# A two-layer encoder kernel: a thirteenth feed-forward chunk by seven half-size products, shared PSUM banks, x kept in DRAM, some low parts added by DMA out of HBM

## The chip, the cores and the metric

The kernel runs on one core of one Trainium2 chip. A core has a matrix engine (TensorE, PE in the profile; its weight loads are PEld), VectorE (DVE), ScalarE (ACT), GpSimd (POOL) and SyncE (SP), which work side by side, each on a queue of its own in order, and 16 DMA engines. Data lie in HBM (also called DRAM here), in the core's SBUF, and in PSUM, eight banks of 128 x 512 fp32 values into which TensorE writes. The metric is the device time of one execution in microseconds (us), the median of several; lower is better.

## What is computed

x is 512 tokens by 1024 features, in fp32. Two layers follow each other; the first mixes tokens by a gated linear attention (GLA), the second by softmax attention with rotary positions. Each mixer is followed by a feed-forward part:

```python
for i in range(DEPTH):                      # 2
    h = rmsnorm(x, norm_mix[i])
    x = x + (gla_mixer(h, ...) if i % 2 == 0 else attn_mixer(h, ...))
    x = x + conv_ffn(rmsnorm(x, norm_ffn[i]), ffn_w_up[i], ffn_w_conv[i], ffn_b_conv[i], ffn_w_down[i])

def conv_ffn(h, w_up, w_conv, b_conv, w_down):      # w_up 1024 x 5632, w_down 2816 x 1024
    u = conv3(h @ w_up, w_conv) + b_conv            # depthwise over tokens, width 3
    val, gate = split(u, 2)
    return (silu(gate) * val) @ w_down
```

## The kernel before

**Precision.** Every fp32 operand of a matmul is held as a high part, rounded to the matrix engine's fp32r form, and a low part, the rest. One product is three matmuls: high x high, high x low, low x high (`mm3`, lines 387 to 389, and the loop at 856 and 857). The high part of a weight is a ScalarE copy (line 227), the low part a VectorE subtraction (line 228). `low_dma` (lines 178 to 181) makes the low part in another way: ScalarE writes the high part (179), then its negative, the raw value negated and rounded, into the low tile (180), and an accumulating DMA issued by POOL adds the raw value (`flush`, line 217).

**Tiling.** Features lie on the 128 partitions, 512 tokens on the free axis: x is eight tiles of 128 x 512. The 5632 up-projection features are 22 chunks m, each with a value and a gate tile. A *plain* chunk (`plain_up`) is two tiles of 8 x 3 = 24 matmuls of 512 columns. A chunk in SEVEN (`seven_up`) is done by a Strassen-like scheme: four blocks of weights, token halves of 256 columns, and seven products instead of eight; each product is 4 pairs x 3 = 12 matmuls of 256 columns (`product`, line 848), so a chunk is 84. Sums of weight blocks are made by VectorE (`summed`, lines 187 to 212), sums of input blocks in `prepare_input`. Results are put together in PSUM banks r1 to r5 and the SBUF tiles c and d: ScalarE copies r2<-r1 (line 873) and r3<-r2 (877), VectorE adds. In before, 12 chunks are done this way.

**Down-projection.** 16 of the 22 chunks feed it by seven products as well, in two parts after chunks 9 and 17 (`down_part`), of four strips with 84 matmuls each. Their inputs are pairs of chunks (`prepare`); the pairs in Q_DMA get their low parts by accumulating DMA, the others by VectorE (line 919). The results g and f of a strip are added to x in SBUF by accumulating DMA. The last six chunks are multiplied plainly at the end (PLAIN, `mm3` into `dn`).

**Activation.** `act_up` takes the two results of a chunk through the convolution (ScalarE line 904, VectorE 905 and 906), the gate's SiLU (908) and the product (909).

**Normalisation.** The first SWITCH chunks multiply the un-normalised x (tiles xhl) and are scaled by R behind the matmul (line 845). From chunk SWITCH on, the normalised x is used (tiles nh and nl, made in `rescale` with low parts by accumulating DMA). `prepare_input` runs after the chunks named in INPUT_AT and makes the tiles xt.

**Buffers.** A pool tag has a fixed number of buffers: raw weights NR = 4 (of 128 x 1024), high and low parts NH = NL = 4, u 4, t 6, sq 3; PSUM banks acc 3, s 2, pt 2, po 1. `Weights.piece` makes pieces ahead of their use, as many as PA, UPA or `ahead` say, and loads LOADS further ones ahead on SP.

**Order.** The source gives dependencies and priorities; the tile framework orders each engine's queue when the program is built, by its own cost estimates, and makes an instruction wait where a buffer or an operand is due. So the order in the trace isn't always that of the source. `issue_after` fixes an order by hand.

In the GLA part (lines 465 to 800) each head makes ktl twice (line 633, tag u), kth twice (tag t), at (t), ath and atl (658 and 659, u), then runs 18 kv matmuls and 12 o matmuls (702), copies of kv by line 690, and the next head's projections.

Of the kernel before, what the change touches and what calls it, by code (L numbers as in the profile page):

```python
# [48 lines left out]
SEVEN = (7, 8, 10, 11, 12, 13, 15, 16, 18, 19, 20, 21)  # L49
# [3 lines left out]
SWITCH = 4  # L53
INPUT_AT = {3: (0, 1), 4: (2,), 5: (3,)}
Q_DMA = (2, 4, 5, 6)
NR = 4
NH = 4
NL = 4

# [9 lines left out]
def hybrid_encoder_kernel(  # L69
# [25 lines left out]
    pp = ctx.enter_context(tc.tile_pool(name="pp", bufs=1, space=bass.MemoryType.PSUM))  # L95

# [17 lines left out]
    def tmp(tag, n, w=S):  # L114
        return sp.tile([P, w], F32, tag=tag, bufs={"u": 4, "t": 6, "sq": 3}[tag], name=nm(n))
# [5 lines left out]
    x = [cp.tile([P, S], F32, name=f"x{c}") for c in range(KC)]  # L121
    prm = cp.tile([P, PC_N], F32, name="prm")

    class Weights:
# [3 lines left out]
        def __init__(self):  # L128
            self.todo, self.made, self.by_dma, self.pending = [], {}, [], []
            self.sums, self.last, self.fine = set(), None, []  # L130
            self.loaded, self.strip = {}, {}

        def add(self, src, strips=None, pieces=2):
            for i in strips or range(src.shape[0]):
                order = (0, 1, 3, 2) if pieces > 2 and src.shape[0] == FC else range(pieces)
                self.todo += [(src, i, h) for h in order]
                if pieces > 2:
                    self.sums.add((id(src), i))
# [22 lines left out]
        def make(self, key):  # L161
# [13 lines left out]
        def two(self):  # L175
            return pair("wh", NH, F32R, "wh"), pair("wl", NL, F32R, "wl")

        def low_dma(self, hi, lo, r):
            act.activation(hi, r, AF.Copy)
            act.activation(lo, r, AF.Copy, scale=-1.0)  # L180
            self.pending.append((lo, r))

        def summed(self, src, i, h):
# [3 lines left out]
            a21, a11, a12, a22 = t1[:, :S], t1[:, S:], t3[:, :S], t3[:, S:]  # L187
            if h == 0:
                r = tmp("t", "sum")
                with tc.issue_after(self.last.ins) if self.last else ExitStack():  # L190
                    dve.tensor_tensor(r, a21, a11, ALU.add)
                    dve.tensor_tensor(a21, a21, a22, ALU.add)
                hi, lo = self.two()
                for sl, y in ((slice(0, S), r), (slice(S, 2 * S), a11)):
                    act.activation(hi[:, sl], y, AF.Copy)
                    dve.tensor_tensor(lo[:, sl], y, hi[:, sl].bitcast(F32), ALU.subtract)
                return hi, lo
            if h == 1:
                dve.tensor_tensor(a11, a21, a11, ALU.add)
                hi, lo = self.two()  # L200
                self.split(hi, lo, t1)
                return hi, lo
            if h == 2:
                hi, lo = self.two()
                self.split(hi, lo, t3)
                return hi, lo
            r = tmp("sq", "sum4")
            dve.tensor_tensor(r, a11, a12, ALU.add)
            hi, lo = (sp.tile([P, S], F32R, tag="sq", bufs=3, name=nm(n)) for n in ("wh4", "wl4"))
            act.activation(hi, r, AF.Copy)  # L210
            self.last = dve.tensor_tensor(lo, r, hi.bitcast(F32), ALU.subtract)
            return hi, lo

        def flush(self):

            for lo, r in self.pending:
                pool.dma_start(lo.bitcast(F32), r, accum_op=ALU.add)
# [23 lines left out]
        def ahead(self, n):  # L241
# [3 lines left out]
            for key in self.todo[:LOADS]:  # L245
# [36 lines left out]
    act.dma_start(prm, par)  # L282
    raw = [pair("raw", NR, F32, "first") for i in range(4)]
# [145 lines left out]
    def out_steps(src, hl, nxt, late):  # L429
# [19 lines left out]
        def end(ng):  # L449
            for n in range(2):  # L450
                c = ng * 2 + n
                dve.tensor_tensor(x[c], x[c], pss[ng][n], ALU.add)
                nxt.chunk(c)

# [10 lines left out]
    def gla(norm, nxt):  # L465
# [58 lines left out]
        rst = sp.tile([P, S], F32R, tag="t", bufs=6, name="rst")  # L524
# [77 lines left out]
        def f32r(tag, n):  # L602
            return sp.tile([P, S], F32R, tag=tag, bufs={"u": 4, "t": 6}[tag], name=nm(n))
# [770 lines left out]
```

## Time and profile before

| what | value |
|---|---|
| time, median of 3 runs | 1098.73 us (1098.07 to 1100.32) |
| the profiled execution's own time | 1098.06 us |
| its span, first to last instruction | 1096.3 us |
| granted TensorE clock | 1.000 |
| GLA and start, to the first up matmul | 0 to 225.9 us |
| feed-forward, layer 0 | 225.9 to 572.6 us |
| attention | 572.6 to 746.0 us |
| feed-forward, layer 1 | 746.0 to 1092.9 us |
| HBM read, written | 100.21 MB, 2.10 MB |

The profile is of one execution. A row of its order of time has the start, the duration, the engine, the line, the operation, what is written and read (buffer numbers left out), the shape, and in brackets the engine's idle time before it and what ended it. A group's row has the count, the busy time and mean duration in ns, and the idle time before such instructions. In a table by windows, each engine has its busy time and the number of its instructions in that stretch (PE, PEld, DVE, ACT, POOL), then the clock, the mean busy share of the DMA engines and GB/s. Matmuls overlap, so their pace is read from their starts.

### The profile page before, as it was taken

The numbers are of one execution on the slowest core, as the hardware profiler recorded it, in microseconds if no ns is written. First come the engines' busy times: TensorE is split into PE (matmuls) and PEld (weight loads), VectorE is DVE, ScalarE is ACT, GpSimd is POOL, SyncE is SP. The second block draws the span as 40 slices with busy tenths as digits, with TensorE's granted clock in tenths as the row PEclk, the third lists the DMA queues.
The fourth block names the chain that finished last, engine by engine and source line by source line (L and its number), as shares of the span: only waits on it lengthen the run. The fifth ranks groups of instructions, "written<-read, shape, count | busy, mean of one in ns | idle before, by whom it ended". The sixth has DMA issues, their size and how long they took to land.

```text
span 1096.3 us, 17577 instructions
## 1 busy us (share of the span) xinstructions
PE 1088.7 (99%) x6644; PEld 975.0 (89%) x6644; DVE 881.3 (80%) x1417; ACT 678.0 (62%) x1158; POOL 143.4 (13%) x158
## 2 busy tenths in 40 slices
PE   9999999999999999999999999999999999999998
PEld 7888888888899999999988888788889999999997
DVE  6686776669989799988955588766998979998892
ACT  6565343447766677666764677745776667766670
POOL 0100123000100211010014343000110021101000
PEclk9999999999999999999999999999999999999999
DMA  7432223236645745364457474433673574536422
GB/s 255 132 98 95 66 70 116 83 101 162 154 111 140 174 121 149 116 164 125 154 137 180 120 227 143 157 111 97 157 163 103 147 171 124 146 111 166 125 95 77
DMA packets 52309, 146.45 MB, mean 134 GB/s; under 512 B 6144, under 2 KB 7680, under 8 KB 52224
## 3 DMA queue, kind: packets, MB, share of 16 engines
q1 hardware_dynamic: 32736, 102.17, 28.5%
q0 software_dynamic: 14592, 34.61, 17.2%
q10 hardware_dynamic: 4896, 8.55, 2.1%
q8 instruction: 52, 0.85, 0.3%
q14 instruction: 33, 0.27, 0.1%
HBM read 100.21 MB, written 2.10 MB: 93 GB/s over the span
## 4 chain that ended last, share of the span: by engine, by line
PE 94%; DVE 2%; ACT 2%; issue 1%; DMA 1%; DVEq 0%; SPq 0%; ACTq 0%
PE r L857 33%; PE vg L419 8%; PE op L445 8%; PE up L387 7%; PE up L388 7%; PE up L389 7%; PE dn L387 2%; PE dn L388 2%; PE dn L389 2%; PE av L419 1%; PE o L713 1%; PE A L387 1%; PE B L387 1%; PE A L389 1%; PE B L389 1%
## 5 line engine op out<-in xcount | busy, mean ns | idle before, releaser
L227 ACT ACTIVATE wh<-raw 128x1024 fp32r<-128x1024 f32 x164 | 171.6, 1055 | 146.7 <-PE op L445 32.1
L228 DVE TENSOR_TENSOR wl<-raw,wh 128x1024 fp32r<-128x1024 f32 x164 | 199.9, 1224 | 46.4 <-ACT wh L227 43.5
L857 PE MATMUL r<-gu,wh 128*128 128x256 f32 x896 | 162.8, 284 | 0.0
L857 PE MATMUL r<-xt,wh 128*128 128x256 f32 x768 | 141.1, 284 | 1.0 <-ACT r L873 1.0
L857 PEld LDWEIGHTS r<-gu,wh 128*128 128x128 f32 x896 | 140.1, 192 | 1.6 <-ACT r L976 0.6
L857 PE MATMUL r<-gu,wl 128*128 128x256 f32 x448 | 126.5, 283 | 0.0
L857 PEld LDWEIGHTS r<-xt,wh 128*128 128x128 f32 x768 | 119.9, 192 | 2.6 <-ACT r L873 1.8
L857 PE MATMUL r<-xt,wl 128*128 128x256 f32 x384 | 108.3, 283 | 0.0
L857 PEld LDWEIGHTS r<-gu,wl 128*128 128x128 f32 x448 | 85.9, 192 | 0.0
L857 PE MATMUL r<-nl,wh 128*128 128x256 f32 x288 | 81.5, 283 | 0.0
L857 PE MATMUL r<-nh,wl 128*128 128x256 f32 x288 | 81.5, 283 | 0.0
L857 PE MATMUL r<-nh,wh 128*128 128x256 f32 x288 | 81.5, 283 | 0.0
L419 PE MATMUL vg<-wh,xhl 128*128 128x512 f32 x256 | 79.7, 390 | 1.1 <-DVE wh L225 1.1
L387 PE MATMUL up<-nh,wh 128*128 128x512 f32 x192 | 74.9, 390 | 0.0
L388 PE MATMUL up<-nl,wh 128*128 128x512 f32 x192 | 74.9, 390 | 0.0
L389 PE MATMUL up<-nh,wl 128*128 128x512 f32 x192 | 74.7, 389 | 0.0
L857 PEld LDWEIGHTS r<-xt,wl 128*128 128x128 f32 x384 | 73.5, 192 | 0.0
L445 PE MATMUL op<-oT,wh 128*128 128x512 f32 x256 | 72.1, 394 | 0.0
L419 PEld LDWEIGHTS vg<-wh,xhl 128*128 128x128 f32 x256 | 48.0, 188 | 11.2 <-ACT sq L361 1.3
L445 PEld LDWEIGHTS op<-oT,wh 128*128 128x128 f32 x256 | 47.4, 188 | 9.7 <-ACT oT L741 0.3
L857 PEld LDWEIGHTS r<-nl,wh 128*128 128x128 f32 x288 | 55.3, 192 | 0.2
L857 PEld LDWEIGHTS r<-nh,wh 128*128 128x128 f32 x288 | 55.3, 192 | 0.2
(279 smaller groups left out, 2745.2 us busy)
## 6 DMA issues: line engine op xcount, KB each, us to landing
raw<-in_w_up_dram SPq DMA_DIRECT2D x84, 512.0 KB, 3.9
raw<-in_w_down_dram SPq DMA_DIRECT2D x44, 512.0 KB, 4.1
wl<-raw POOLq DMA_DIRECT2D x16, 512.0 KB, 4.9
raw<-in_w_vg_dram SPq DMA_DIRECT2D x12, 512.0 KB, 3.9
ring<-p ACTq DMA_DIRECT2D x22, 256.0 KB, 2.9
raw<-in_w_kq_dram SPq DMA_DIRECT2D x8, 512.0 KB, 3.6
raw<-in_w_gout_dram SPq DMA_DIRECT2D x8, 512.0 KB, 3.6
nl<-xr POOLq DMA_DIRECT2D x8, 512.0 KB, 5.3
```

Source lines behind the costliest of these rows:

```text
L227: act.activation(hi[:, sl], r[:, sl], AF.Copy)
L228: dve.tensor_tensor(lo[:, sl], r[:, sl], hi[:, sl].bitcast(F32), ALU.subtract)
L387: mm(ps, wh, mh, start=start, stop=False)
L388: mm(ps, wh, ml, start=False, stop=False)
L389: return mm(ps, wl, mh, start=False, stop=stop)
L419: mm(ps[j][:, :width], hl[k][i == 2][:, j * P : (j + 1) * P], (wl if i == 1 else wh)[:, sl], start=k == 0 and i == 0, stop=k == KC - 1 and ...
L445: mm(pss[ng][n], wt[:, sl], mv, start=k == 0 and i == 0, stop=k == KC - 1 and i == 2)
L713: last = mm(og[s], l, r, start=False, stop=i == len(parts) - 1, skip_group_check=True)
L857: mm(dst, w[:, sl], m, start=start and j == 0 and a == 0, stop=j == len(pairs) - 1 and a == 2, skip_group_check=True)
```

## The change

- Chunk 6 joins SEVEN (13 chunks). SWITCH and INPUT_AT move one chunk earlier.
- The seven products use another set of block sums with other signs, so that subtractions take the place of some scaled ones. A strip's third sum is one VectorE operation of 1024 into a raw buffer; there are three splits of 1024 and one of 512.
- Results share banks: r1 and r2 are the halves of one acc bank. The first product goes to a pt bank, and ScalarE copies it into both halves (`twice`). r3 is a whole s bank, whose halves are two copies of r2 at two moments. One VectorE addition of 512 makes d. The convolution reads the other result in PSUM, and c is gone. The order of the products is 1, 6, 7, 4, 5, (1 of the next chunk), 2, 3; before it was 1, 6, 7, 3, 5, 4, (1), 2 for up chunks and 1, 6, 7, 5, 4, 3, (1), 2 for down strips.
- The low parts of the plain chunks 1, 2 and 5 are made by `low_dma`, and the accumulating DMA reads the raw weights in HBM (UP_DMA). Q_DMA is empty: the low parts of those pairs go to VectorE.
- x is saved to DRAM by SP as the mixer's output projection ends (`x_save`), and the down parts are accumulated there. Its four SBUF buffers hold every third piece of weights from chunk 1 to 20 (`wide`), with more pieces ahead (PAW = 6). At chunk 20 x is loaded back (`x_load`).
- Buffers: raw 5 for 4, u 3 for 4, t 5 for 6. In the attention, copies of probabilities go to a raw buffer, and one rotary tile to the tag R.

```diff
-SEVEN = (7, 8, 10, 11, 12, 13, 15, 16, 18, 19, 20, 21)
+SEVEN = (6, 7, 8, 10, 11, 12, 13, 15, 16, 18, 19, 20, 21)
-SWITCH = 4
-INPUT_AT = {3: (0, 1), 4: (2,), 5: (3,)}
-Q_DMA = (2, 4, 5, 6)
-NR = 4
+SWITCH = 3
+INPUT_AT = {2: (0, 1), 3: (2,), 4: (3,)}
+Q_DMA = ()
+UP_DMA = (1, 2, 5)
+NR = 5
+LOADS_FFN = 3
+WIDE_AT, BACK_AT = 1, 20
+PAW, UPAW = 6, 3
...
-        return sp.tile([P, w], F32, tag=tag, bufs={"u": 4, "t": 6, "sq": 3}[tag], name=nm(n))
+        return sp.tile([P, w], F32, tag=tag, bufs={"u": 3, "t": 5, "sq": 3}[tag], name=nm(n))
...
+    def x_save(p):
+        if p == 0:
+            x_home[:] = [dp.tile([P, 2 * S], F32, tag=nm("xd"), name=nm("xd")) for _ in range(KC // 2)]
+        for i in range(2):
+            sync.dma_start(x_home[p][:, i * S : (i + 1) * S], x[2 * p + i])
+    def x_load():
+        for home, t in zip(x_home, x_tiles()):
+            sync.dma_start(t, home)
...
+            elif any(src is a and i in UP_DMA for a in up):
+                self.low_dma(hi, lo, r, src[i, :, h * 2 * S : (h + 1) * 2 * S].bitcast(F32R))
...
         def two(self):
+            self.turn += self.wide
+            if self.wide and self.turn % 3 == 0:
+                return pair("x", KC // 2, F32R, "wh"), pair("x", KC // 2, F32R, "wl")
             return pair("wh", NH, F32R, "wh"), pair("wl", NL, F32R, "wl")
...
+            if h == 1:
+                e = pair("raw", NR, F32, "sum")
+                self.strip[id(src), i].append(e)
+                both = lambda t: t.rearrange("p (o n) -> p o n", n=S)
+                with tc.issue_after(self.last.ins) if self.last else ExitStack():
+                    dve.tensor_tensor(both(e), both(a21).to_broadcast([P, 2, S]), both(t1), ALU.subtract)
+                dve.tensor_tensor(a21, a11, e[:, S:], ALU.subtract)
+            hi, lo = self.two()
+            self.split(hi, lo, self.strip[id(src), i][h])
...
         def seven_up(m):
-            r1 = bank("acc", "r1")[:, :H]
-            go(1, r1, True)
-            r2 = bank("acc", "r2")[:, :H]
-            act.activation(r2, r1, AF.Copy)
+            r = bank("pt", "r1")[:, :H]
+            go(1, r, True)
+            both = bank("acc", "r")
+            r1, r2 = both[:, :H], both[:, H:]
+            twice(both, r)
             yield
             go(6, r2, False)
-            r3 = bank("s", "r3")[:, :H]
-            act.activation(r3, r2, AF.Copy)
+            r3 = bank("s", "r3")
+            act.activation(r3[:, :H], r2, AF.Copy)
             r4 = bank("pt", "r4")[:, :H]
             go(7, r4, True)
-            r5 = bank("pt", "r5")[:, :H]
-            go(3, r5, True)
+            d = tmp("u", "u")
+            twice(d, r4)
+            go(4, r3[:, :H], False)
             go(5, r2, False)
...
-            go(4, r3, False)
+            act.activation(r3[:, H:], r2, AF.Copy)
+            add_seven(d, r3, r4)
+            yield 1, d
             begin_up(m + 1)
             go(2, r1, False)
-            dve.tensor_tensor(d[:, :H], d[:, :H], r3, ALU.subtract)
-            yield 1, d
-            act.activation(c[:, :H], r1, AF.Copy)
-            yield 0, c
+            go(3, r2, False)
+            yield 0, both
...
+        def twice(d, r4):
+            two = lambda a: a.rearrange("p (o t) -> p o t", t=H)
+            act.activation(two(d), two(r4).to_broadcast([P, 2, H]), AF.Copy)
+        def add_seven(d, r3, r4):
+            dve.tensor_tensor(d, d, r3, ALU.add)
...
         for m in range(FC):
+            if m == BACK_AT:
+                W.loads, W.wide = LOADS, 0
+                x_load()
+            elif m == WIDE_AT:
+                W.loads, W.wide = LOADS_FFN, 1
             held.append(act_up(m))
```

`down_part` is changed in the same way as `seven_up`; there a strip's two results go by ScalarE to f and g and are accumulated into x_home.

More of the change, by code (lines that the diff above doesn't have):

```diff
@@ L131, in __init__ @@
             self.loaded, self.strip = {}, {}
+            self.loads, self.wide, self.turn = LOADS, 0, 0
         def add(self, src, strips=None, pieces=2):
             for i in strips or range(src.shape[0]):
[L135 to L136 removed]
+                self.todo += [(src, i, h) for h in range(pieces)]
                 if pieces > 2:
@@ L183, in summed @@
         def summed(self, src, i, h):
             t1, t3 = self.strip[id(src), i][:2]
[L187 to L196, printed above, removed]
+            a11, a21, a12 = t1[:, :S], t3[:, :S], t3[:, S:]
@@ L828, in plain_up @@
                 ps = bank("s" if t else "acc", "up")
-                feature_tile(*W.half(up[layer], 2 * m + t, max(UPA, ahead.get((m, t), 1))), norm.hl if m < SWITCH else fresh, ps)
+                feature_tile(*W.half(up[layer], 2 * m + t, max(UPAW if W.wide else UPA, ahead.get((m, t), 1))), norm.hl if m < SWITCH else fresh, ps)
                 pss.append(ps)
@@ L850, in product @@
             if h not in pieces:
-                pieces[h] = W.piece(src, strip, h, PA)
+                pieces[h] = W.piece(src, strip, h, PAW if W.wide else PA)
             wh, wl = pieces[h]
```

114 lines of the change are left out of this document (52 added, 62 removed).

## The prediction

> **What bounds the kernel now.** I read the page first (busy shares, then the chain that ended last), then TensorE's waits, then its order of time.
>
> ```profile
> span 1096.3 us, 17577 instructions
> ...
> PE 1088.7 (99%) x6644; PEld 975.0 (89%) x6644; DVE 881.3 (80%) x1417; ACT 678.0 (62%) x1158; POOL 143.4 (13%) x158
> ...
> PE 94%; DVE 2%; ACT 2%; issue 1%; DMA 1%; DVEq 0%; SPq 0%; ACTq 0%
> ```
>
> The chain runs through TensorE for 94% of the span: the time is the number of matmuls times their pitch, plus what TensorE waits. Waits come next; columns are who waited for whom, us in total, times, longest.
>
> ```profile
> PE r L857 <- ACT r L873: 1.0, 2, 0.5
> ```
>
> It is the only wait of note in the two feed-forward stages: once in each layer a product waits for ScalarE's copy r2<-r1. A busy row overlaps its neighbours (284 ns for a 256-column matmul), so I take the pitch from first starts in the order of time:
>
> ```profile
> 238.07 0.48 PE L387 MATMUL up<-xhl,wh 128*128 128x512 f32 x1
> ...
> 298.02 0.28 PE L857 MATMUL r<-nh,wh 128*128 128x256 f32 x1
> ...
> 336.00 0.28 PE L857 MATMUL r<-gu,wh 128*128 128x256 f32 x1
> ...
> 409.79 0.28 PE L857 MATMUL r<-nh,wl 128*128 128x256 f32 x1
> 410.60 0.39 PE L857 MATMUL r<-xt,wh 128*128 128x256 f32 x1 [0.53 <-ACT r L873]
> ...
> 416.43 0.40 PE L387 MATMUL up<-nh,wh 128*128 128x512 f32 x1
> ...
> 929.88 0.28 PE L857 MATMUL r<-nh,wl 128*128 128x256 f32 x1
> 930.68 0.39 PE L857 MATMUL r<-xt,wh 128*128 128x256 f32 x1 [0.52 <-ACT r L873]
> ```
>
> Between 238.07 and 298.02 stand plain chunks 1 to 5 and one tile of 6, 11 x 24 = 264 matmuls of 512 columns: 59.95 / 264 = 0.2271 us each. Between 336.00 and 416.43 stand four down strips and chunks 10 to 13: 8 x 84 less the 12 of the first product, done ahead, is 660 matmuls of 256 columns. The start gap at 409.79 is 0.81, which is 0.69 over a pitch of 0.12; (80.43 - 0.69) / 660 = 0.1208 us. In layer 1 the same wait costs 0.80 - 0.12 = 0.68.
>
> **The change part by part.** *Chunk 6 by seven products.* Plain: 48 x 0.2271 = 10.90 us; seven: 7 x 12 x 0.1208 = 10.15. It saves 0.75 a layer, **-1.50 us**. No other edit changes the number of matmuls, so the rest counts by waits alone.
>
> *The wait for r2<-r1.* Now ScalarE copies r1 out of its own bank into both halves of the shared one, and two products (2 and 3 of the chunk before, 2 x 1.45 = 2.9 us) lie between it and its reader, in place of one. Why it was late:
>
> ```profile
> 406.00:416.40 10.40, 9.88 (x82) 9.67 (x82) 9.54 (x17) 9.95 (x19) 2.93 (x4) 1.00 0.97 233
> ```
>
> ScalarE (the second figure of 9.9 with x19) was busy 9.95 of 10.40 us, with the negated copies of line 180 for pair 6. Q_DMA is empty now, so these go too. I count both waits gone: 0.69 + 0.68, **-1.37 us**. Next late are the copies below.
>
> *VectorE, ScalarE, POOL.* Prices:
>
> ```profile
> L228 DVE TENSOR_TENSOR wl<-raw,wh 128x1024 fp32r<-128x1024 f32 x164 | 199.9, 1224 | 46.4 <-ACT wh L227 43.5 <-issue 1.3 <-PE r L857 1.3
> L227 ACT ACTIVATE wh<-raw 128x1024 fp32r<-128x1024 f32 x164 | 171.6, 1055 | 146.7 <-PE op L445 32.1 <-DVE raw L199 30.1 <-PE up L388 26.5
> ...
> L196 DVE TENSOR_TENSOR wl<-sum,wh 128x512 fp32r<-128x512 f32 x40 | 27.5, 688 | 10.0 <-ACT wh L195 9.4
> ...
> L886 DVE TENSOR_TENSOR u<-u,r 128x256 f32<-128x256 f32 x24 | 9.9, 414 | 0.0
> ...
> L179 ACT ACTIVATE gu<-y 128x512 fp32r<-128x512 f32 x16 | 10.0, 625 | 3.4 <-DVE y L909 3.2
> ```
>
> VectorE, a layer, with 1.22, 0.69 and 0.41 us for 1024, 512 and 256 columns. Six low halves go to DMA, -7.3. Four prepared pairs return from it, 4 x (3 x 0.69 + 0.41) = +9.9. A strip costs 4 x 1.22 + 3 x 0.69 = 6.95 in place of 2 x 1.22 + 7 x 0.69 = 7.27, on 20 strips -6; chunk 6 as a strip is +4.5. Results cost one add of 512 (0.69) in place of three of 256 (1.24), -6.6 on 12 chunks, +0.7 for chunk 6, -1 on the down strips. SWITCH drops two scalings, -1.4. Sum about -7 us. ScalarE, by the 1.06 and 0.63 us rows: +6.3 for the six negated copies, -9 for the pairs, -4 on strips, +3.6 for chunk 6, -2 on results, +3.7 down: about -1. Neither is on the path while pieces are ready, and the lookahead grows from four pairs of buffers to six: **0 us**, but it is what hides these engines. POOL issues 6 accumulations more and 16 fewer a layer. x goes out and back 2 MB a layer on SP; x_load waits there until the four borrowed buffers are free and holds up the loads queued behind it, late in chunk 21, when the first down halves are in the raw buffers already: 0.
>
> *Copies with less cover.* Line 877's copy r3<-r2 had two to three products between its source (6) and its reader (4); now only product 7. And r1 and r2 share a bank. What that means shows where kv halves share one:
>
> ```profile
> 139.89 0.28 PE L389 MATMUL kv<-vrh,ktl 128*128 128x256 f32 x1
> ...
> 140.24 0.28 PE L389 MATMUL kv<-vrh,ktl 128*128 128x256 f32 x1
> ...
> 140.56 0.38 ACT L690 ACTIVATE sa<-kv 128x256 f32<-128x256 f32 x1 [0.68 <-PE kv L389]
> ```
>
> ScalarE reads the half that was done at 139.89 + 0.28 = 140.17, idles, and starts at 140.56, just after the other half's last matmul (140.24 + 0.28). So products 2 and 3 must wait for the second copy, r3's right half <- r2 after product 5, though 2 writes the other half. The Trainium skill (PSUM — Partial Sum Buffer, section "PSUM bank collisions raise a hardware error") asks for the same: guard by bank, not by address; the trace agrees, and that rule speaks against this part of the change. The price goes by bounds:
>
> ```profile
> 347.95 0.37 ACT L985 ACTIVATE r<-r 128x256 f32<-128x256 f32 x1 [0.87 <-PE r L857]
> ```
>
> Where ScalarE is waiting already, the copy follows its product at once and ends 0.37 us later, in a cover of 1.45: nothing is lost. Upper end: 13 + 8 strips in two layers with two such copies are 84. Before, 16 places a layer had one product of cover and lost 1.37 together, 0.043 each, so 76 cost 3.3; after chunks 8, 13, 16 and 21 no begun chunk covers the second copy, 8 x about 0.6 = 4.8 if nothing else is put in. But other work is put in: the queue order bends around a late operand:
>
> ```profile
> 175.91 0.28 PE L702 MATMUL o<-vrl,ath 128*128 128x256 f32 x1
> 176.03 0.28 PE L702 MATMUL o<-vrh,ath 128*128 128x256 f32 x1
> 176.26 0.39 PE L702 MATMUL o<-vrh,atl 128*128 128x256 f32 x1
> ```
>
> Here the third matmul by source order (atl) comes behind a later one with ath, since atl was late. I take **+0.2** (0 to +8.1), by the row at 347.95.
>
> *Three u tiles in place of four.* A GLA head holds four (two ktl, ath, atl). Now atl waits until the first ktl is read, by the ninth kv matmul, which is the third in front of the 139.89 row above (starts 139.53, ends 139.8). In front of it on VectorE:
>
> ```profile
> 139.64 1.22 DVE L228 TENSOR_TENSOR wl<-raw,wh 128x1024 fp32r<-128x1024 f32 x1 [0.17 <-ACT wh L227]
> ...
> 140.96 0.28 PE L702 MATMUL o<-vrh,atl 128*128 128x256 f32 x1
> ```
>
> atl would end at 140.8 + 0.69 = 141.5 and is due at 140.96: 0.55 in three heads, 1.7, less what later ath matmuls fill. If VectorE is free at 139.8 it is nothing. I take **+0.2** (0 to +1.7). The t tiles (five for six) have a free one by then.
>
> *The low parts of chunks 1, 2, 5, and SWITCH.* The critical one is the second half of chunk 2:
>
> ```profile
> 246.75 1.04 ACT L227 ACTIVATE wh<-raw 128x1024 fp32r<-128x1024 f32 x1
> ...
> 252.41 0.87 POOL L217 DMA_DIRECT2D nl<-xr  x1 [1.56 <-ACT nl L180]
> ...
> 254.96 0.39 PE L389 MATMUL up<-xhl,wl 128*128 128x512 f32 x1
> ```
>
> The first is ScalarE's high part, the second the last accumulation for the normalised x, the third the half's first use of its low part. The landing times of those accumulations (the view of the tile nl):
>
> ```profile
> DMA to landing us min/median/max: 4.6/5.3/7.5
> ```
>
> The DMA share (1.02) in that stretch, in the table by windows:
>
> ```profile
> 249.00:260.00 11.00, 11.00 (x50) 9.09 (x50) 11.00 (x18) 7.89 (x11) 1.72 (x2) 1.00 1.02 224
> ```
>
> The high part starts at 246.75, the negated copy would end at 248.8, and an accumulation issued then lands 4.6 to 7.5 us later: 253.4 to 256.3, against a first use at 254.96. The median leaves 0.8. The normalised x's low parts, due a chunk earlier by SWITCH, land last at 252.41 + 7.5 = 259.9; the last pair's first use is in chunk 3, six 128-row steps after its start: 238.07 + 96 x 0.2271 + 19 x 0.2271 = 264.2. I take **0** (0 to +8 a layer, below). HBM latency under load is up to 2 us in the Trainium skill (DMA: Bandwidth & Descriptors, section "Latency and other measured facts"); no run here shows an accumulation out of HBM. By that figure, an estimate, this half would land at about 256.1 and cost 1.2 us a layer, and the sum would be 2.4 us higher.
>
> Sum: -1.50 - 1.37 + 0.2 + 0.2 = -2.5 us on the profiled execution (1096.3 span, 1.8 around it, 1098.06 in all). The median of three is 1098.73, 0.67 above it, and the comparison is with such a median: 1098.73 - 2.5 = **1096.2 us**.
>
> **The rivals.** *The covers give it back (same).* The copies after products 6 and 5, and atl, cost 2 to 3 us of their 9.8: 1098.5. For: ScalarE's 1.06 us copies stand in the same queue and can't be interrupted. Against: only two late copies in 32 so far. That chunk 6 gains nothing (a piece of it late on a VectorE that is full from 249 to 260) ends here too: 1097.7.
>
> *The low parts land late (slower).* One mechanism: in 249 to 260 the DMA engines are full (share 1.02), and another 0.5 MB accumulation goes among four. The queue that accumulates:
>
> ```profile
> q0 software_dynamic: 14592, 34.61, 17.2%
> ```
>
> 0.172 x 1096.3 = 188.6 us for 34.61 MB, so 2.9 us for 0.52 MB. Behind the last nl it would land at 259.9 + 2.9 = 262.8, 7.8 us late; behind one or two of them, about 3. It decides from an issue later than 254.96 - 5.3 = 249.7. At 3 us a layer the time is 1102.2, at the end of the bound 1111.8. For: full engines and a slack of 0.8 us. Against: POOL could issue it at 248.8, ahead of two nl.
>
> *All covers hold (faster).* 1098.73 - 2.87 = 1095.9; runs of before lie down to 0.7 below their median (1098.07), so 1095.2.
>
> **How the numbers follow.** Forecast with all covers holding or nearly so 0.43; gain given back 0.27; low parts late or another feed missed 0.30. A difference of 0.2% (2.2 us) is about what a measurement of this kernel can tell from none. Faster 0.43, same 0.27, slower 0.30. The likeliest case's own range is 1095.2 to 1096.5. The range of 8 in 10 goes from 1094.9 to 1103.0, the slower rival at 3 us a layer and a little; beyond it stay its worst end, 0.13, and 0.05 below.
>
> **What would show it.** Right: chunk 6 takes 10.15 us; no wait of TensorE for line 873's successor. Copies: waits of product 4 or 2 for ScalarE. GLA: o waits for atl at 121, 141, 161. Low parts: TensorE's up waits for a DMA at 249 to 265 and 769 to 785. Wrong altogether: pieces late, seen as r waiting for VectorE's wl.

## The result and the profile after

| | before | after |
|---|---|---|
| median of 20 runs | 1099.81 us (1098.07 to 1100.61) | 1096.97 us (1095.75 to 1098.75) |
| the profiled execution's own time | 1098.06 us | 1096.11 us |
| its span | 1096.3 us | 1094.0 us |

The ratio is 0.9979, 95% interval 0.9973 to 0.9985: the kernel after is faster by 2.8 us, where 2.5 was forecast. (1096.2 was forecast from the first median of before, 1098.73; all 20 runs of it have 1099.81.) The runs of each kernel fall in two groups 1.6 to 1.9 us apart and the two medians lie in different groups; group by group the kernel after is faster by 2.3 us (medians 1098.49 and 1096.19) and by 2.0 us (1100.10 and 1098.13). The page of the kernel after, with the rows that answer to those of before (span; busy time by engine; the chain that ended last):

```profile
span 1094.0 us, 17377 instructions
...
PE 1086.3 (99%) x6716; PEld 975.8 (89%) x6716; DVE 870.8 (80%) x1301; ACT 683.1 (62%) x1086; POOL 126.6 (12%) x138
...
PE 96%; DVE 2%; ACT 1%; DMA 1%; issue 0%; SPq 0%; DVEq 0%; ACTq 0%
```

TensorE has 72 matmuls more (2 x 36: 84 of 256 columns for 48 of 512 in chunk 6, twice) and is busy 2.4 us less. VectorE loses 10.5 us and ScalarE gains 5; with TensorE at 99% neither shows directly. TensorE's waits in the kernel after (line waited for, us in total, times, longest):

```profile
PE r L879 <- ACT r L907: 0.7, 1, 0.7
PE o L724 <- DVE atl L681: 0.3, 2, 0.2
...
PE pt L1257 <- DMA ring<-p: 0.2, 1, 0.2
```

The old row (L857 for L873, 1.0 in two places) is gone; three new ones stand here, the last in the attention. Which stage each us came from is read from first starts in the order of time: first up matmul, first matmul of the attention, last up or down matmul. "Waits" in the table are the gaps between all starts of TensorE in a feed-forward part, each less the pitch of its width (0.227 or 0.120 us), added up.

| us | first up matmul at | layer 0 feed-forward (waits in it) | attention | layer 1 feed-forward (waits) | span |
|---|---|---|---|---|---|
| before | 225.88 | 346.69 (2.28) | 173.43 | 346.49 (2.31) | 1096.3 |
| after | 226.90 | 344.13 (0.54) | 173.63 | 345.51 (2.14) | 1094.0 |
| difference | +1.02 | -2.56 (-1.74) | +0.20 | -0.98 (-0.17) | -2.3 |

A layer's matmuls without their waits take 344.41 and 344.18 us before, 343.59 and 343.37 after: 0.8 less in each. That 0.8 is the counts times the two pitches (48 x 0.227 - 84 x 0.120), so it is no measurement of its own. This is one: in layer 0, from the first up matmul to the first product of a down strip, both kernels have the same matmuls but for chunk 6 and the same two gaps of 0.1 us, and the stretch takes 103.22 us before (225.88 to 329.10) and 102.46 after (226.90 to 329.36), 0.76 less. The rest is waits: 1.74 us of them gone in layer 0, next to none in layer 1, and 1.0 us more ahead of the feed-forward.

Layer 1 lost most of its gain in one place, shown by the order of time (start, duration, instruction; in brackets the idle time before it and what ended it). First TensorE, then ScalarE, both of the kernel after:

```profile
829.98 0.28 PE L879 MATMUL r<-nh,wl 128*128 128x256 f32 x1
830.24 0.50 PE L879 MATMUL r<-xt,wh 128*128 128x256 f32 x2
831.45 0.38 PE L879 MATMUL r<-nh,wh 128*128 128x256 f32 x1 [0.71 <-ACT r L907]
```

```profile
828.18 1.06 ACT L247 ACTIVATE wh<-raw 128x1024 fp32r<-128x1024 f32 x1 [1.21 <-DVE raw L228]
829.14 1.04 ACT L247 ACTIVATE wh<-sum 128x1024 fp32r<-128x1024 f32 x1
830.09 1.04 ACT L247 ACTIVATE wh<-raw 128x1024 fp32r<-128x1024 f32 x1
831.04 0.36 ACT L907 ACTIVATE r<-r 128x256 f32<-128x256 f32 x1
```

Product 2 waits for the second copy out of the shared bank. That copy takes 0.36 us, but stands behind three copies of a weight piece, and the first of those had waited 1.21 us for a sum from VectorE. In this queue, which runs in order, one late operand was passed on to all behind it. Layer 0 has the same program, and there this place shows no wait.

Ahead of the feed-forward the new wait is that for atl, twice the same (at 121.65 and 141.63); VectorE first, then TensorE:

```profile
120.22 1.23 DVE L248 TENSOR_TENSOR wl<-raw,wh 128x1024 fp32r<-128x1024 f32 x1 [0.17 <-ACT wh L247]
121.36 0.69 DVE L681 TENSOR_TENSOR atl<-at,ath 128x512 fp32r<-128x512 f32 x1
```

```profile
121.53 0.28 PE L724 MATMUL o<-vrh,ath 128*128 128x256 f32 x1
121.65 0.28 PE L724 MATMUL o<-vrl,ath 128*128 128x256 f32 x1
122.10 0.39 PE L724 MATMUL o<-vrh,atl 128*128 128x256 f32 x1 [0.17 <-DVE atl L681]
122.32 0.28 PE L724 MATMUL o<-vrh,ath 128*128 128x256 f32 x1
```

The start gap is 0.45, so 0.33 over the pitch, and the gap behind it 0.22 in place of 0.12: with the second head about 0.85 us, most of the 1.02.

The low parts out of HBM cost TensorE nothing. Landing times of accumulations (KB each, median us from issue to landing, DMA view of the kernel after; the third row is the normalised x's, out of SBUF and in the same stretch), the issue for the second half of chunk 2, that half's first use, and two windows: the 277 matmuls from the first up matmul on, before and after.

```profile
wl<-raw POOLq DMA_DIRECT2D x16, 512.0 KB, 5.2
...
wl<-in_w_up_dram POOLq DMA_DIRECT2D x12, 512.0 KB, 7.9
...
nl<-xr POOLq DMA_DIRECT2D x8, 512.0 KB, 7.9
```

```profile
241.02 0.88 POOL L237 DMA_DIRECT2D wl<-in_w_up_dram  x1 [5.48 <-ACT wl L206]
...
255.98 0.39 PE L410 MATMUL up<-xhl,wl 128*128 128x512 f32 x1
```

```profile
225.88:287.14 61.26, 61.26 (x277) 50.83 (x276) 54.96 (x91) 41.02 (x54) 7.15 (x8) 1.00 0.55 139
```

```profile
226.90:288.16 61.26, 61.26 (x277) 50.84 (x276) 52.71 (x90) 49.05 (x62) 12.37 (x14) 1.00 0.91 205
```

Issued at 241.02 it lands, by the median, at about 248.9, 7 us ahead of its use. The stretch takes 61.26 us in both kernels, although the DMA engines went from 0.55 to 0.91 busy.

### The profile page after: what moved, and what is told of

Same layout as the page of the kernel before. It is cut to its first block, busy times and chain, and to the rows that moved or that the text cites. A ratio compares the mean times of both kernels' runs of the same rounds, so it can differ in the third digit from the quotient of the medians.

```text
span 1094.0 us, 17377 instructions
## 1 busy us (share of the span) xinstructions
PE 1086.3 (99%) x6716; PEld 975.8 (89%) x6716; DVE 870.8 (80%) x1301; ACT 683.1 (62%) x1086; POOL 126.6 (12%) x138
## 4 chain that ended last, share of the span: by engine, by line
PE 96%; DVE 2%; ACT 1%; DMA 1%; issue 0%; SPq 0%; DVEq 0%; ACTq 0%
PE r L879 37%; PE vg L440 8%; PE op L466 8%; PE up L408 6%; PE up L409 6%; PE up L410 6%; PE dn L409 2%; PE dn L410 2%; PE dn L408 2%; PE av L440 1%; PE o L735 1%; PE A L408 1%; PE A L409 1%; PE A L410 1%; PE B L410 1%; PE B L408 1%
## 5 line engine op out<-in xcount | busy, mean ns | idle before, releaser
L248 DVE TENSOR_TENSOR wl<-raw,wh 128x1024 fp32r<-128x1024 f32 x152 | 185.2, 1220 | 34.1 <-ACT wh L247 33.9
L247 ACT ACTIVATE wh<-raw 128x1024 fp32r<-128x1024 f32 x152 | 158.5, 1052 | 84.4 <-PE op L466 22.6
L879 PE MATMUL r<-xt,wh 128*128 128x256 f32 x832 | 151.2, 283 | 0.0
L879 PEld LDWEIGHTS r<-xt,wh 128*128 128x128 f32 x832 | 130.1, 192 | 0.5 <-ACT wh L247 0.2
L879 PE MATMUL r<-xt,wl 128*128 128x256 f32 x416 | 117.4, 283 | 0.0
L879 PE MATMUL r<-nh,wh 128*128 128x256 f32 x312 | 88.9, 285 | 0.7 <-ACT r L907 0.7
L879 PE MATMUL r<-nh,wl 128*128 128x256 f32 x312 | 88.3, 283 | 0.0
L879 PE MATMUL r<-nl,wh 128*128 128x256 f32 x312 | 88.3, 283 | 0.0
L879 PEld LDWEIGHTS r<-xt,wl 128*128 128x128 f32 x416 | 79.7, 192 | 0.0
L879 PEld LDWEIGHTS r<-nh,wl 128*128 128x128 f32 x312 | 59.8, 192 | 0.0
```

Of the source, the lines that this page charges most:

```text
L247: act.activation(hi[:, sl], r[:, sl], AF.Copy)
L248: dve.tensor_tensor(lo[:, sl], r[:, sl], hi[:, sl].bitcast(F32), ALU.subtract)
L879: mm(dst, w[:, sl], m, start=start and j == 0 and a == 0, stop=j == len(pairs) - 1 and a == 2, skip_group_check=True)
```

## The experiments

**The theory** after the result: time is matmuls plus TensorE's waits, and the waits went because ScalarE and VectorE run further ahead (borrowed buffers, pairs off ScalarE, low parts off VectorE), not because a single wait was cut. Each part that feeds the lookahead should then cost more to undo than its own wait was worth. **The rivals**: chunk 6 alone is the gain; the wait went by its second product of cover alone; the DMA parts do nothing.

### Chunk 6 alone, on the kernel before

```diff
-SEVEN = (7, 8, 10, 11, 12, 13, 15, 16, 18, 19, 20, 21)
+SEVEN = (6, 7, 8, 10, 11, 12, 13, 15, 16, 18, 19, 20, 21)
-SWITCH = 4
-INPUT_AT = {3: (0, 1), 4: (2,), 5: (3,)}
+SWITCH = 3
+INPUT_AT = {2: (0, 1), 3: (2,), 4: (3,)}
```

> The kernel before with one part of the change alone: chunk 6 by seven products, SWITCH and INPUT_AT one chunk earlier. Theory (the other parts are what feeds it): VectorE is full from 238 to 293 us and must now make a strip of 7.27 us for chunk 6 in place of 2.45 us of low parts, so pieces come late and TensorE waits; slower than before by some 3 us (ratio 1.001 to 1.008), with waits of r or up for VectorE's low parts before 330 us. Rival (the matmul count alone rules): 1.50 us faster, ratio 0.9986, no new wait.

Measured: 1103.72 us, ratio 1.0048 (1.0035 to 1.0062); waits in the two feed-forward parts 7.96 and 3.56 us. TensorE's waits of this run, and the place:

```profile
PE r L857 <- DMA xt<-xr: 4.3, 2, 3.6
```

```profile
299.13 0.46 PE L857 MATMUL r<-xt,wh 128*128 128x256 f32 x1 [3.62 <-DMA xt<-xr]
```

By itself the chunk that saves 1.5 us of matmuls makes the kernel 5 us slower. Sign and size are within what the theory gave, but the late thing is another than I named: not a weight piece but the low part of a sum of inputs, which chunk 6 needs a chunk sooner. The wait also cost more than itself: behind it TensorE ran at half the granted clock for 3.4 us (the figure ahead of the last two), starts 0.21 us apart in place of 0.12, another 1.6 us.

```profile
299.40:302.70 3.30, 3.30 (x17) 3.30 (x17) 1.90 (x4) 1.41 (x4) 0.00 (x0) 0.50 0.00 0
```

### The kernel after without chunk 6

```diff
-SEVEN = (6, 7, 8, 10, 11, 12, 13, 15, 16, 18, 19, 20, 21)
+SEVEN = (7, 8, 10, 11, 12, 13, 15, 16, 18, 19, 20, 21)
```

> The changed kernel with chunk 6 plain again. Theory: 48 x 0.2271 against 84 x 0.1208 us, so each feed-forward part is 0.75 us longer than in the changed kernel and the whole 1.5 us, ratio to before 0.9992. Rival (chunk 6 costs waits that eat its gain): within 0.5 us of the changed kernel.

Measured: 1098.17 us, ratio 0.9991 (0.9982 to 1.0000). Layer 0 takes 346.19 us (waits 1.78), layer 1 345.31 (1.12). Without waits that is 344.41 and 344.19, 0.8 more in each layer, which is the count times the pitch again. The wait at 830 us is gone, others of 0.2 to 0.6 us are new. Against before the other parts alone take 1.7 us of waits out (2.90 for 4.59). The interval of the ratio overlaps that of the kernel after (0.9973 to 0.9985), so the runs alone don't separate the two.

### No borrowed buffers

```diff
-                W.loads, W.wide = LOADS_FFN, 1
+                W.loads, W.wide = LOADS_FFN, 0
```

> The changed kernel without the borrowed buffers (x still goes to DRAM and back, but no weights lie in its place; four pairs of buffers, shorter lookahead). Theory of the prediction (the lookahead hides VectorE and ScalarE): TensorE waits for pieces of weights in the seven-product chunks, 3 to 10 us slower than the changed kernel, ratio to before 1.001 to 1.007. Rival (four pairs do, as they did before): within 0.5 us of the changed kernel, ratio 0.997 to 0.999.

Measured: 1102.55 us, ratio 1.0033 (1.0020 to 1.0046): 5.6 us slower than after. Waits are 4.69 and 4.68 us, 44 gaps over 25 ns in each layer against 4 and 14:

```profile
PE r L879 <- ACT wh L247: 1.0, 4, 0.2
PE r L879 <- DVE wl L248: 0.4, 2, 0.2
...
PE r L879 <- ACT r L934: 0.3, 2, 0.2
```

No row is long, and these rows are under a fifth of the sum: the rest is many small delays of pieces, what a short lookahead looks like. This is the largest single loss of the parts undone, and the prediction had put the buffers at 0 us.

### Pairs by DMA again

```diff
-Q_DMA = ()
+Q_DMA = (2, 4, 5, 6)
```

> The changed kernel with Q_DMA back at (2, 4, 5, 6): ScalarE again makes the negated copies of four pairs a layer. Theory A (ScalarE's load made the copy late): waits of r for ScalarE of 0.5 us and more come back near chunks 12 to 14, 1 to 2 us slower than the changed kernel. Theory B (the cover of two products takes them away): no such wait, within 0.3 us of the changed kernel.

Measured: 1100.02 us, ratio 1.0007 (0.9998 to 1.0016); waits 3.37 and 2.33 us. TensorE's waits, then ScalarE's order of time at one of the three places, then TensorE's:

```profile
PE r L879 <- ACT r L900: 1.9, 3, 0.7
```

```profile
432.96 0.40 ACT L205 ACTIVATE gu<-b 128x256 fp32r<-128x256 f32 x1
433.27 0.40 ACT L206 ACTIVATE gu<-b 128x256 fp32r<-128x256 f32 x1
433.57 1.43 ACT L922 ACTIVATE y<-up,cw 128x512 f32<-128x512 f32 x2
434.90 0.62 ACT L219 ACTIVATE wh<-raw 128x512 fp32r<-128x512 f32 x1
435.42 0.37 ACT L900 ACTIVATE r<-r 128x256 f32<-128x256 f32 x1
```

```profile
434.96 0.28 PE L879 MATMUL r<-nh,wl 128*128 128x256 f32 x1
435.85 0.38 PE L879 MATMUL r<-xt,wh 128*128 128x256 f32 x1 [0.61 <-ACT r L900]
```

With the negated copies (L206) back, ScalarE is busy without a break and its copy is late again, but not the one that was late before: r1's copy now has two products of cover and is never late; r3<-r2 (L900), which has one, takes the wait over. That fits both halves of my reason: the load makes the lateness, the cover decides which copy shows it.

### Low parts by VectorE again

```diff
-UP_DMA = (1, 2, 5)
+UP_DMA = ()
```

> The kernel after, with the low parts of up chunks 1, 2 and 5 made by VectorE again instead of by the accumulating DMA out of HBM. Six subtractions of 1.22 us come back to VectorE in each layer, all of them in the 61.26 us between the first up matmul and 288.16 us, where VectorE is busy for 52.71 us (0.86). Theory (the DMA buys VectorE time that TensorE then doesn't wait for): VectorE stands at about 59 us of 61.3 there and every hiccup reaches TensorE, 0.5 to 2 us more in each layer, a ratio to the kernel before of 0.999 to 1.0015. Rival (the low parts are made early enough by either means, and what the DMA relieves is off the path): within 0.3 us of the kernel after, a ratio of 0.997 to 0.9985, and no wait of TensorE between 227 and 290 us.

Measured: 1098.71 us, ratio 0.9994 (0.9985 to 1.0002). Layer 0 346.00 us (waits 2.41), layer 1 345.44 (2.07); TensorE's waits:

```profile
PE r L879 <- DMA xt<-xr: 0.5, 1, 0.5
PE r L879 <- DVE wl L248: 0.5, 2, 0.3
```

The median is 1.7 us above after, with intervals that just touch. In the one profile it is the theory's size in layer 0 (+1.9 us) and none in layer 1, where other small waits took the place of the one at 830. And not where expected: there is no wait while those low parts are used. It comes 8 to 25 us after the window, at 296.0 (0.69 over the pitch) and 313.1 us (0.48), for a sum of inputs and a weight piece. VectorE's row for the window shows why it isn't where I looked:

```profile
226.80:288.06 61.26, 61.26 (x278) 50.83 (x277) 55.17 (x92) 40.90 (x53) 7.16 (x8) 1.00 0.57 138
```

It is busy 55.2 us and not the 59 that I had added up (52.7 with the DMA): most of the 7.3 us pushed other work out of the window, by my reading that for the chunks by seven.

### r1 and r2 in banks of their own

```diff
-            both = bank("acc", "r")
-            r1, r2 = both[:, :H], both[:, H:]
-            twice(both, r)
+            r1, r2 = bank("acc", "r1")[:, :H], bank("acc", "r2")[:, :H]
+            act.activation(r2, r, AF.Copy)
+            act.activation(r1, r, AF.Copy)
...
+            c = tmp("u", "u")
+            act.activation(c[:, :H], r1, AF.Copy)
             go(3, r2, False)
-            yield 0, both
+            act.activation(c[:, H:], r2, AF.Copy)
+            yield 0, c
```

> The kernel after, with r1 and r2 in two banks of their own and the finished pair copied out to SBUF by ScalarE as before, all thirteen seven-product chunks kept. Theory (the shared bank is what lets the second copy stop TensorE at 830.46 us for 0.87 us, since product 2 may not write the bank while ScalarE reads it): that wait goes, product 2 writes r1 in its own bank; about 0.9 us faster than the kernel after, a ratio of about 0.997. Rival (the shared bank pays by sparing ScalarE the copies of the pair and PSUM a bank): two more copies per chunk and the second accumulation bank taken bring waits of TensorE for ScalarE or for a bank, 1 to 4 us slower than the kernel after, a ratio of 0.999 to 1.0015.

Measured: 1097.66 us, ratio 0.9982 (0.9973 to 0.9991), no different from after. The wait at 830 is gone, and three smaller ones came:

```profile
PE r L879 <- ACT r L900: 0.6, 3, 0.3
```

Waits 0.77 and 1.80 us in place of 0.54 and 2.14. The shared bank is what exposes the second copy; taken by itself, sharing neither pays nor costs.

### atl in other buffers

```diff
-            return sp.tile([P, S], F32R, tag=tag, bufs={"u": 3, "t": 5}[tag], name=nm(n))
+            return sp.tile([P, S], F32R, tag=tag, bufs={"u": 3, "t": 5, "sq": 3}[tag], name=nm(n))
-        hi, lo = f32r("u", "ath"), f32r("u", "atl")
+        hi, lo = f32r("u", "ath"), f32r("sq", "atl")
```

> The kernel after, with the low part of the attention weights in the first stage (atl, L681) put in the three buffers of tag sq instead of the three of tag u, which ktl and the high part share. Theory (the fourth u buffer that the change took is what makes atl late in two of the three heads with little to fill): the two waits of 0.33 us at 121.65 and 141.63 us go with the slow pitch behind each, 0.8 us less before the first up matmul, a ratio of about 0.9972 where the kernel after has 0.9979. Rival (atl is late by VectorE's queue, the wl piece of 1.23 us ahead of it, and not by the buffer): no difference, first up matmul at 226.9 us as in the kernel after.

Measured: 1094.95 us in 5 runs, ratio 0.9963 (0.9950 to 0.9975). The first up matmul starts at 225.71, 1.19 us sooner than after; the two feed-forward parts are the same (344.13, 345.47). VectorE, then TensorE where it had waited:

```profile
118.42 0.69 DVE L681 TENSOR_TENSOR atl<-at,ath 128x512 fp32r<-128x512 f32 x1 [0.70 <-ACT ath L680]
```

```profile
121.49 0.28 PE L724 MATMUL o<-vrh,atl 128*128 128x256 f32 x1
```

The buffer was the cause, by way of the queue: with a buffer of its own atl stands at 118.42, ahead of the wl piece, as it does before (118.33); in the kernel after it stood behind that piece, at 121.36. Matmul by matmul 0.84 us of the 1.19 come at the two waits, as expected; 0.3 come between 180 and 189 us, behind the last head, and no run gives their cause. The stage's gain is shown; the total's is less sure, since five runs happened to lie close together where other kernels spread over 3 us (below).

### The second copy removed, or given to VectorE

The left half added last, so that VectorE takes the right half straight from r2 (on the kernel after):

```diff
-            r3 = bank("s", "r3")
-            act.activation(r3[:, :H], r2, AF.Copy)
+            r3 = bank("s", "r3")[:, :H]
+            act.activation(r3, r2, AF.Copy)
...
-            go(4, r3[:, :H], False)
             go(5, r2, False)
-            act.activation(r3[:, H:], r2, AF.Copy)
-            add_seven(d, r3, r4)
+            add_seven(d[:, H:], r2, r4)
+            go(4, r3, False)
+            add_seven(d[:, :H], r3, r4)
```

> The kernel after, with the products of an up chunk in the order 6, 7, 5, 4: after product 5 VectorE adds the right half straight from r2, after product 4 the left half from r3, and the second copy of ScalarE (L907) is gone in all thirteen chunks of both layers; VectorE gets two additions of 256 columns for one of 512. Theory (the one wait of 0.87 us at 830.46 us is for that second copy, held up in ScalarE's queue): it goes, and nothing takes its place, 0.9 us faster than the kernel after, a ratio of about 0.9971. Rival (products 2 and 3 now wait for VectorE's read of r2, and VectorE is the busier engine, 0.92 busy between 288 and 540 us): waits of TensorE for the additions in several chunks, 1 to 4 us slower than the kernel after.

The same copy by VectorE (on the kernel with atl moved):

```diff
-            act.activation(r3[:, H:], r2, AF.Copy)
+            dve.tensor_copy(r3[:, H:], r2)
```

> The kernel of the run with atl in the other buffers, and the second copy of an up chunk, right half of r3 from r2 (L907), made by VectorE instead of ScalarE. Theory (the wait of 0.87 us before product 2 comes from ScalarE's queue, in which three copies of 1.04 us stood ahead of that copy): it goes, and the copy costs VectorE under half a us in each of 26 places, 0.9 us faster than the kernel with atl in the other buffers, first up to last matmul 0.9 us shorter. Rival (VectorE, 0.92 busy in the chunks by seven, holds the copy up as much): waits of TensorE before product 2 for VectorE in one or several chunks, 1 to 4 us slower than that kernel.

Measured: 1099.74 us, ratio 1.0003 (0.9994 to 1.0012), waits 3.05 and 2.45; and 1105.31 us, ratio 1.0063 (1.0048 to 1.0078), waits 5.70 and 4.69. TensorE's waits of the first, then of the second:

```profile
PE r L879 <- ACT r L900: 1.4, 2, 1.0
...
PE r L879 <- ACT r L934: 0.5, 1, 0.5
```

```profile
PE up L408 <- ACT u L934: 1.3, 1, 1.3
...
PE up L408 <- DVE y L924: 0.8, 1, 0.8
```

The wait at 830 went in both, so its cause is right. On the price the first rival is right (2.8 us over the kernel after); the second asked too little, 1 to 4 us, where 7.8 us of waits came on top and the median rose by 10. In the first, TensorE hardly waits for VectorE's reads as the rival had it; it waits for the copies L900 and L934 instead. In the second, TensorE hardly waits for the copy itself; VectorE's load shows up in the convolution (L924) and beyond. Every such edit also re-orders the queues, since the framework plans them from its own costs; which copy ends up behind which piece wasn't separated from the edit itself.

### Low parts of chunks 3 and 4 too

```diff
-UP_DMA = (1, 2, 5)
+UP_DMA = (1, 2, 3, 4, 5)
```

> The kernel after, with the low parts of up chunks 3 and 4 as well made by the accumulating DMA out of HBM, ten halves in a layer instead of six. Theory (the DMA rings are what bounds this form: 0.91 of them busy between 227 and 288 us, 7.9 us to landing where 5.2 was seen from SBUF): four more transfers of 512 KB, each read and written, land late, TensorE waits for low parts between 240 and 290 us, 2 to 8 us more in each layer, a ratio to the kernel before of 1.002 to 1.012. Rival (the landing time is mostly latency and the queue has room): no wait, VectorE 5 us less busy in each layer, within 0.5 us of the kernel after, a ratio of 0.997 to 0.9985.

Measured: 1108.47 us, ratio 1.0084 (1.0071 to 1.0097). Landing, the waits, the window, and the longest wait:

```profile
wl<-in_w_up_dram POOLq DMA_DIRECT2D x20, 512.0 KB, 9.1
```

```profile
PE up L410 <- DMA wl<-in_w_up_dram: 9.5, 4, 6.6
```

```profile
226.80:288.00 61.20, 58.27 (x260) 47.34 (x259) 47.27 (x83) 51.16 (x64) 15.82 (x18) 1.00 0.98 221
```

```profile
783.16 0.39 PE L409 MATMUL up<-nl,wh 128*128 128x512 f32 x1
790.12 0.79 PE L410 MATMUL up<-nh,wl 128*128 128x512 f32 x1 [6.57 <-DMA wl<-in_w_up_dram]
```

This is the slower rival of the prediction, brought about by four more halves: DMA share 0.98, landing 9.1 us in the median, and TensorE stands. After the longest wait it ran for another 3 us at a granted clock of 0.50, which cost 1.5 us more. Six halves a layer fit here, ten don't.

### The pause ahead of the first weights

On the kernel with atl moved, twice:

```diff
+    more = bank("po", "more")            # first run; bank("s", "more") in the second
+    for i in range(3):
+        mm(more[:, :P], two[:, :P], two[:, P : 2 * P], start=i == 0, stop=i == 2)
```

> The kernel of the run with atl in the other buffers, and three more of the eight small products that TensorE runs ahead of the first weights (L324), into a bank of their own. The runs of every kernel so far fall in two groups some 1.7 us apart, and in the profiles of the later group TensorE ran the first eight matmuls of 512 columns, 6.1 to 9.7 us, at a pitch of 0.427 us instead of 0.227. Theory (TensorE comes to full speed after a stretch of work without a pause, and the pause of 1.0 us between the last small product and the first vg matmul sometimes spoils that): without the pause the later group is gone, all runs within 1 us of each other, a median of 1094.5 to 1095.5 us. Rival (which group a run falls in is settled by something else): two groups as before, about half of the runs 1.7 us later.

> As the run before with three more small products, which came too late there: they shared their bank with the first eight, so that TensorE ran them at 8.19 us, behind the first four vg matmuls and the pause. Here they have another bank (tag s) and stand right behind the eight, where TensorE otherwise pauses for 1.0 to 1.3 us; otherwise the kernel with atl in the other buffers. Theory (the pause spoils the coming to full speed in part of the runs): all runs within 1 us of each other, median 1094.5 to 1095.5 us, ratio to the kernel before 0.995 to 0.9965, and the first vg matmuls at a pitch of 0.227 us. Rival (which group a run falls in is settled by something else): two groups 1.6 us apart, a median between 1095 and 1097 us.

The first, 1098.41 us, ratio 0.9994 (0.9985 to 1.0003), says nothing of its theory: its products ran behind the pause. It says something else: attention and layer 1 took 1.4 and 1.5 us longer than in the kernel it was made from, with TensorE's matmuls in the same order there, so that one profile doesn't settle a difference of that size. The second: 1097.01 us in 12 runs, ratio 0.9979 (0.9968 to 0.9990), from 1094.79 to 1099.93 with a gap between 1097.4 and 1098.4. The pause is gone and the rival holds: two groups stay. What decides between them is open; the last section has what the profiles show of it. The six runs from 1097.44 us on have a mean granted clock of 0.998, the six below 0.999 or 1.000; where they lost it no trace here shows. With atl moved and the same chunks, this run starts its first up matmul at 226.07 and has 344.13 and 345.61 us of feed-forward.

No run undoes by themselves the new block sums, the order of the products, the single addition for d or the way of x through DRAM.

## Why the prediction was right, and where it wasn't

- **Chunk 6, -1.50.** Right: 0.76 us in layer 0 by direct reading, for 0.75. That no feed would be missed was right only because of the other parts; on the kernel before it loses 5 us.
- **The wait for r2<-r1, -1.37.** Right that both go. Too small in what goes with it: layer 0 lost 1.74 us of waits, of which this wait and the slow pitch behind it are 0.79; the rest are small waits of 0.04 to 0.15 us that I hadn't counted, at the starts of products and strips.
- **Copies with less cover, +0.2.** The mis-sized term: 0 in layer 0, and 0.87 in one place of layer 1, 1.2 with the small gaps around it. The row at 347.95 was a fair guide for nearly all of the 84 copies; the one that failed stood behind pieces of 1.04 us, which the "same" rival had named. The places without a begun chunk, priced at up to 4.8, show at most 0.2 us each (the last one of a layer, at 536.8 and 1056.1).
- **Three u tiles, +0.2.** Mechanism right to the instruction (the wl piece of 1.23 us ahead of atl, two heads with too little to fill), size too small: 0.85. Its working gave 0.55 a head; I took off too much for filling.
- **Low parts out of HBM, 0.** The number was right and the argument wrong. The row at 246.75 that I took for the second half of chunk 2 makes the first half of chunk 3; the half in question is made at 238.71 after and issued at 241.02, so the slack was 7 us, not 0.8. The landing time was wrong too, 7.9 us for an assumed 5.3. The Trainium skill gives an HBM latency of up to 2 us at high load (DMA: Bandwidth & Descriptors, section "Latency and other measured facts"); the extra 2.7 us over the SBUF source of the other weights (5.2) is more than that. The source need not be the reason: the accumulations for the normalised x (nl), out of SBUF, rose from 5.3 to 7.9 us in the same stretch, where the DMA engines went from 0.55 to 0.91 busy. But those for xt, out of SBUF too and a little later, stayed at 5.2, so the runs don't split the source from the load. The two errors, in slack and in landing time, had opposite signs. The chance of 0.30 for "slower" stood mostly on the wrong row.
- **VectorE, ScalarE, lookahead, 0.** The loads came out at -10.5 us for VectorE and +5.1 for ScalarE in both layers together, where I had added up about -14 and -2. The price of 0 held only in sum. Undone one by one the parts cost 5.6 (buffers), 3 (pairs) and 1.7 us (low parts), by medians; for the last the intervals just touch. They were not on the path, but they feed what is.
- **x to DRAM and back, 0.** No wait of TensorE for x shows in any trace here. The attention's 0.20 us had no term in the forecast; it is the size of its new wait for a DMA (ring<-p).

The sum: -0.81 - 0.81 for the matmuls, -1.74 and -0.17 for the waits, +1.02 and +0.20 elsewhere is -2.3, the difference of the spans. The forecast had -2.5 with smaller terms on both sides: the feed-forward waits fell by 0.7 us more than it said (1.91 for 1.17), and the rest gave 1.0 us more back (1.22 for 0.2). That these two errors nearly cancel is luck. The single waits came about as described, except for the low parts; what the lookahead was worth is what the sum left out.

## What to carry to other kernels

In a kernel with one engine at 99%, price a change by that engine's work plus its waits; work saved counts only if the feeding engines can follow, so ask of each part what it feeds, and test a saving by itself before believing it. A short copy is as late as the queue that it stands in: look at what is ahead of it, not at its own 0.36 us. And when a slack is read from rows, make sure which piece the row belongs to by counting pieces from the first.

## What the runs showed of the hardware that was not expected

- An accumulating DMA of 512 KB out of HBM lands in 7.9 us (median of 12), with ten a layer in 9.1; out of SBUF it lands in 5.2 (median of 16, weights of the attention), but in 7.9 (of 8) for the normalised x in the same stretch.
- After a long wait TensorE came back at half clock. In the run with chunk 6 alone, 3.62 us of idling were followed by 3.4 us at a granted clock of 0.50; in the run with ten halves the clock fell during the wait of 6.57 us and stayed at 0.50 for 3 us behind it. The other waits in these traces, of up to 1.8 us, show no such drop.
- After a wait TensorE's next start comes about 0.1 us late as well (122.10 to 122.32, for a pitch of 0.12), so many small waits cost more than they look.
- In five of the fourteen profiles TensorE ran its first eight or more matmuls of 512 columns at half pace. First of the kernel after, then of the run with r1 and r2 in own banks (four matmuls a row):

```profile
5.99 1.16 PE L440 MATMUL vg<-wh,xhl 128*128 128x512 f32 x4 [1.01 <-DVE wh L245]
6.99 1.09 PE L440 MATMUL vg<-wl,xhl 128*128 128x512 f32 x4
```

```profile
6.13 2.05 PE L440 MATMUL vg<-wh,xhl 128*128 128x512 f32 x4 [1.06 <-DVE wh L245]
7.98 1.48 PE L440 MATMUL vg<-wl,xhl 128*128 128x512 f32 x3
```

Four starts take 1.00 us in the one and 1.85 in the other. That moves the first up matmul by 1.6 us (226.90 and 228.51), and the spread of one kernel's runs is of that size. Whether the one makes the other wasn't shown; the profile of the run with the second copy by VectorE has the slow start and is the fastest of its six runs. The windows print a granted clock of 1.00 there because the trace has no record of the clock ahead of the first grant of full speed; that grant stands at 4.8 us in the first of the two and at 9.9 in the second, where the half pace ends. The Trainium skill (TensorE: Matmul & The Clock Gate, section "Part 1: The HAM clock gate (the "warmup" mystery)") has a window of about 3.4 us that runs freely and must be busy before TensorE leaves half speed, so that the moment varies from run to run. The trace agrees: 0.427 us a matmul at first and 0.227 afterwards, nearly twice as fast. In the last run, without a pause from the first small product at 1.3 us on, full pace came at 7.1 us, within two such windows. By that rule the pause can cost a window but closing it leaves the phase to chance, which would fit the spread that stayed; no run here sets the phase.
